# The keys' reciprocal norms written straight into their tile, and GpSimd's powers priced higher in a build-time order

## The chip, the cores and the metric

One NeuronCore of a Trainium2 chip runs the whole program. It has five engines that run side by side, each through its own list of instructions and strictly in order: TensorE (PE in the profile, with its weight loads as PEld), VectorE (DVE), ScalarE (ACT), GpSimd (POOL) and SyncE (SP), which here only issues transfers. An instruction that waits holds up everything behind it on its own engine. The metric is the device time of one execution in microseconds (us); lower is better.

## The reference

One block of a transformer on 1024 tokens of width 1024, all in fp32. The input is normed and projected; four heads go through a gated delta rule (a chunked linear recurrence), eight heads through a dilated sliding window attention; both are joined by an output projection, and a gated feed-forward layer of width 2816 follows. The change sits in the norms of the delta-rule heads:

```python
def l2norm(x):
    return x * lax.rsqrt(jnp.sum(x * x, axis=-1, keepdims=True) + 1e-6)

q = l2norm(heads(q)) * GDN_HEAD_DIM ** -0.5
k = l2norm(heads(k))
...
o = chunk_gated_delta_rule(q, k, v, g, beta)
o = o * lax.rsqrt(jnp.mean(o * o, axis=-1, keepdims=True) + RMS_EPS) * onorm_g.astype(f32)
```

## The kernel before, in words

**Who sets the order.** The kernel is written as generators ("strands"), each of which yields one instruction after the other. At build time a class named Weaver picks, step by step, the strand whose next instruction can start earliest by its own running clocks, and writes that instruction into its engine's list. The clocks advance by a cost that class Op gives to each instruction (from line 184 on), plus fixed lags between engines. Nothing of this runs on the chip: only the lists remain. So a cost that is altered alters no instruction by itself, but it alters which one is written next, and from there on every later choice can differ. Some operations are also given to one of two engines by the same clocks (Either: a cast on ACT or DVE, a sum on DVE or GpSimd).

**The stages, in order of time.** (1) The projections: each 128-column block of w_in is split into a high and a low fp32r part, and PE does three matmuls 128x512 for each of eight blocks of the depth (tiles pj). They run through the first 487 us and serve as the filler of all other work on PE in that time. (2) Beside them, for each delta-rule head: a causal convolution on DVE (tile yc, four instructions on 128x1024), the norms of queries and keys (post_q, post_k), and the chunk matrices (intra; tiles rhd, am, attnT on DVE, pm on PE). (3) When all four heads are done, inverse solves 31 triangular steps on DVE (tiles tm and X), then solve finishes on PE. (4) chain, the recurrence over 16 half-tiles: matmuls p1, p2, p3 (p in the profile), DVE tiles R, o and state in between, and for each token tile chain_out, which norms the result (tile on_r). (5) The window attention runs beside the chain, unit by unit: scores on PE (pS), bias and row minimum on DVE (Sr, mx), the exponential on ACT, four transposes on PE (tp<-ident,Sr), their split into high and low parts on ACT and DVE (ptn, pto, ptf), the product with the values on PE (pV), and two sums on DVE (plow, ptmp). (6) The output projection (pw), then the feed-forward layer (bank), which fills the second half of the time.

**The norms.** rstd_from takes sums of squares, scales them on DVE (tile ..._m) and raises them to the power -0.5 on GpSimd (tile ..._r). It is called with the tags rk (keys, 128x4, twice a head), rq (queries, 128x8, once a head), on (the chain's result, 128x4, eight times), and n3 and n4 (norms around the output projection, 128x1, sixteen times). Op prices a power at 295 + 165 n ns for n elements in a row. In post_k the result of rk is first copied on DVE into the tile rk, which holds the norms of all heads, then multiplied in place by a decay (edec), and that product scales the keys (kn).

Of the kernel before, what the change touches and what calls it, by code (L numbers as in the profile page):

```python
# [11 lines left out]
F32 = mybir.dt.float32  # L12
# [3 lines left out]
ALU = mybir.AluOpType  # L16
# [5 lines left out]
P = 128  # L22
# [8 lines left out]
EPS = 1e-6  # L31
# [508 lines left out]
def block_kernel(ctx: ExitStack, tc: tile.TileContext, a, out):  # L540
    nc = tc.nc
    w = Weaver(nc)
    T, V, A, G, SY = (Engine(w, e, k) for e, k in (
        (nc.tensor, "PE"), (nc.vector, "V"), (nc.scalar, "A"), (nc.gpsimd, "G"), (nc.sync, "S")))
# [5 lines left out]
    def tr(out, in_):  # L550
        return T.transpose(out, in_, ident[:])
# [16 lines left out]
    def pool(stack, name, bufs, space=None, side=None):  # L568
        return Pool(w, stack, tc, name, bufs, space, side)
# [11 lines left out]
    mhalf = pc.tile([P, 32], F32, name="mhalf")  # L581

    psums = pc.tile([P, NT, AH], F32, name="psums")

    def rstd_from(pool, ss, scale, eps, tag, bufs=4):
        n = ss.shape[-1]
        m = pool.tile([P, n], F32, name=tag + "_m", bufs=bufs)
        yield V.tensor_scalar(m[:], ss, scale, eps, ALU.mult, ALU.add)
        r = pool.tile([P, n], F32, name=tag + "_r", bufs=bufs)
        yield G.tensor_tensor(r[:], m[:], mhalf[:, :n], ALU.pow)  # L590
        return r

    d_kq = dr.tile([NT, P, GH, 4, 64], F32, name="d_kq")
# [23 lines left out]
    rq = pgv.tile([P, GH, NT], F32, name="rq")  # L617
# [245 lines left out]
    pk = pool(s1, "pk", 2)  # L863
# [30 lines left out]
    rk = pl.tile([P, GH, NT], F32, name="rk")  # L894
    edec = pl.tile([P, 32], F32, name="edec")
# [83 lines left out]
    def conv(raw, wi):  # L979
        raw, used = raw  # L980
        yc = yield pk.get([P, S], F32, name="yc", bufs=1)
        yield V.tensor_scalar(yc[:], raw[:, 0:S], convw[:, wi, 0:1], None, ALU.mult)
        for j in range(1, 4):
            yield V.scalar_tensor_tensor(yc[:], raw[:, j:j + S], convw[:, wi, j:j + 1], yc[:], ALU.mult, ALU.add)
        used.fire()
        return yc

    def tok_major(src, b, after):
        yield After(after)
        tp = yield pt.get([P, 4, P], F32, name="tp")  # L990
        yield [tr(tp[:, k, :], src(4 * b + k)) for k in range(4)]
        return tp

    def sumsq(tp, ss):
        sq = yield pk.get([P, 4, P], F32, name="sq4", bufs=1)
        yield A.activation(sq[:], tp[:], AF.Square)
        yield V.tensor_reduce(ss, sq[:], AX.X, ALU.add)
        pk.put(sq)
# [4 lines left out]
    def post_k(h, raw, evs):  # L1003

        for e in evs:
            yield e
        yc = yield from conv(raw, 4 + h)
        ys = yield pk.get([P, S], F32, name="ys")
        yield A.activation(ys[:], yc[:], AF.Silu)
        pk.put(yc)  # L1010
        kq = kqs[h] = yield pk.get([P, NT, 4, 64], F32, name="kq")
        y4 = ys[:].rearrange("p (t c j) -> p t c j", t=NT, c=2)
        yield Either(A.copy(kq[:, :, 0::3, :], y4), V.tensor_copy(kq[:, :, 0::3, :], y4))
        yield ev_dec
        kn = yield pk.get([P, NT, P], F32, name="kn")
        for b in range(2):
            sl = slice(4 * b, 4 * b + 4)
            tp = yield from tok_major(lambda k: ys[:, k * P:(k + 1) * P], b, ys[:])
            ss = pk.tile([P, 4], F32, name="ssk")
            yield from sumsq(tp, ss[:])  # L1020
            r = yield from rstd_from(pk, ss[:], 1.0, 1e-6, "rk")
            yield V.tensor_copy(rk[:, h, sl], r[:])
            yield V.tensor_tensor(r[:], r[:], edec[:, h * 8 + 4 * b:h * 8 + 4 * b + 4], ALU.mult)
            yield V.tensor_tensor(kn[:, sl, :], tp[:], r[:].unsqueeze(2).broadcast_to([P, 4, P]), ALU.mult)
            pt.put(tp)
        pk.put(ys)
        yield V.tensor_tensor(nbeta[:, h, :], nbeta[:, h, :], rk[:, h, :], ALU.mult)
        yield V.tensor_tensor(nbeg[:, h * 8:h * 8 + 8], nbeg[:, h * 8:h * 8 + 8], rk[:, h, :], ALU.mult)
        ev_k[h].fire()
        yield SY.dma_start(d_kd[:, :, h, :].rearrange("t p d -> p t d"), kn[:])  # L1030
        pk.put(kn)

    def post_q(h, raw, evs):
        for e in evs:
            yield e
        yc = yield from conv(raw, h)
        while h not in kqs:
            yield ev_k[h]
        kq = kqs[h]
        yield A.activation(kq[:, :, 1:3, :], yc[:].rearrange("p (t c j) -> p t c j", t=NT, c=2), AF.Silu)  # L1040
        pk.put(yc)
        ev_q[h].fire()
        ssq = pk.tile([P, 8], F32, name="ssq")
        for b in range(2):
            tp = yield from tok_major(lambda k: kq[:, k, 1:3, :], b, kq[:])
            yield from sumsq(tp, ssq[:, 4 * b:4 * b + 4])
            pt.put(tp)
        rr = yield from rstd_from(pk, ssq[:], 1.0, 1e-6, "rq")
        yield V.tensor_scalar(rq[:, h, :], rr[:], P ** -0.5, None, ALU.mult)
        yield ev_k[h]  # L1050
        yield SY.dma_start(d_kq[:, :, h, :, :].rearrange("t p c j -> p t (c j)"),
                           kq[:].rearrange("p t c j -> p t (c j)"))
        ev_kq[h].fire()
# [202 lines left out]
    def main():  # L1256
# [11 lines left out]
        for n, (kind, i) in enumerate(order):  # L1268
            if kind in ("k", "q", "v"):
                if n < 2:  # L1270
                    raw, ev = pair[n]
                else:
                    raw, ev = (yield from new_raw()), []
                    for hf in range(2):
                        e = yield from proj_half(base[kind] + i, hf, raw_sink(raw))
                        ev.append(e)
                if kind == "k":
                    ev_post.append(w.spawn(post_k(i, raw, ev), 3))
                elif kind == "q":
                    fin += [w.spawn(post_q(i, raw, ev), 3), w.spawn(intra(i), 3)]  # L1280
                    if i == GH - 1:
                        w.spawn(inverse(fin), 2)
                else:
                    ev_post.append(w.spawn(post_v(i, raw, ev), 4))
                    if i == GH - 1:
                        ev_main_v.fire()
            elif n == 2:
                continue
            elif kind == "bv":
                yield from proj_v(i)  # L1290
            elif kind == "gate":
                if i < 2:
                    yield from gate(i)
                elif i == 2:
                    yield from gate(2, 3)
            else:
                yield from proj_qk(base[kind], i, (ev_q2 if kind == "bq" else ev_k2)[i])
# [63 lines left out]
    ch = pool(sc, "ch", 2)  # L1361
# [28 lines left out]
    def chain():  # L1390
        for t in range(NT):
# [4 lines left out]
            for c in range(2):  # L1396
# [30 lines left out]
                cp.put(p2)  # L1427
            ch.put(kq, gg, kd, bv)
            w.spawn(chain_out(o, t), 3)

    def chain_o1(o, p1, sw, us):
# [4 lines left out]
    def chain_out(o, t):  # L1436
        sq = yield ch.get([P, GH, P], F32, name="osq", tag="ot", bufs=1)
        yield A.activation(sq[:], o[:], AF.Square)
        ss = ch.tile([P, GH], F32, name="oss")
        yield V.tensor_reduce(ss[:], sq[:], AX.X, ALU.add)  # L1440
        ch.put(sq)
        yield V.tensor_tensor(ss[:], ss[:], rqs2[:, t::8], ALU.mult)
        r = yield from rstd_from(ch, ss[:], 1.0, EPS, "on", 2)
        yield V.tensor_tensor(r[:], r[:], rqsw[:, t::8], ALU.mult)
        yield V.tensor_tensor(o[:], o[:], r[:].unsqueeze(2).broadcast_to([P, GH, P]), ALU.mult)
        yield After(o[:])
        tp = yield banks.get([P, GH, 2, 64], F32, name="otp")
        yield [tr(tp[:, h, :, :], o[:, h, :]) for h in range(GH)]
        ch.put(o)
        ot = yield ch.get([P, GH, 2, 64], F32, name="ot", bufs=1)  # L1450
        for c in range(2):
            yield A.activation(ot[:, :, c, :], tp[:, :, 1 - c, :], AF.Copy, scale=onorm[:])
        banks.put(tp)
        yield A.dma_start(d_mix[0:4, :, t * P:(t + 1) * P].rearrange("h p j -> p h j"),
                           ot[:].rearrange("p h c j -> p h (c j)"))
        ch.put(ot)
        ev_o[t].fire()
# [1018 lines left out]
```

## Time and the profile before

| | us |
|---|---|
| median of 3 runs (1234.30 to 1237.12) | 1235.44 |
| the profiled execution | 1238.43 |
| its span, first to last instruction | 1236.6 |
| around the span (1238.43 - 1236.6) | 1.8 |
| PE busy | 1212.7 (98%) |
| DVE busy | 967.0 (78%) |
| ACT busy | 573.4 (46%) |
| GpSimd busy | 179.8 (15%) |

The span is what the profile's views cover; the profiled execution lies 3.0 us above the median of the runs. In the views, "x18" counts instructions, the mean duration of one is in ns, and what follows "<-" is what ended an idle time.

### The profile page before, as it was taken

To read this page: it belongs to the slowest core of one execution; us is meant where nothing else is said; L and a number is where in the kernel's file an instruction comes from. 1 tells how busy PE (TensorE), PEld (TensorE's weight loads), DVE (VectorE), ACT (ScalarE), POOL (GpSimd) and SP (SyncE) were. 2 spreads that over 40 slices of the span, in tenths; PEclk is the share of its full clock that TensorE was granted. 3 is DMA by queue.
4 is the path that set the end of the run, shared out by engine and by line. 5 is a ranking of instruction groups with operands and counts; after the bars stand their busy time and mean duration, and the time that the engine had idled before them with its cause. 6 is when DMAs were issued, how large, how long until landed. Compare 5 with 4: busy or idle time off the path is not lost.

```text
span 1236.6 us, 19600 instructions
## 1 busy us (share of the span) xinstructions
PE 1212.7 (98%) x6783; PEld 1013.4 (82%) x6783; DVE 967.0 (78%) x1875; ACT 573.4 (46%) x1162; POOL 179.8 (15%) x153
## 2 busy tenths in 40 slices
PE   8999999999999999999999999999999999999997
PEld 7887798888888877887778888888888888888886
DVE  5689969736998988766898867876678767876886
ACT  6535432236676658555553333333333344544541
POOL 0134321011122111110110010111001100000111
PEclk9999999999999999999999999999999999999999
DMA  8754372778878568785544433322333039645335
GB/s 273 228 158 154 111 227 81 171 228 264 268 224 255 175 185 273 243 275 174 188 134 154 139 128 128 103 65 98 120 128 119 35 120 322 239 131 158 101 121 205
DMA packets 169979, 213.43 MB, mean 173 GB/s; under 512 B 32232, under 2 KB 87016, under 8 KB 169880
## 3 DMA queue, kind: packets, MB, share of 16 engines
q1 hardware_dynamic: 165656, 210.08, 54.0%
q10 hardware_dynamic: 4224, 2.10, 0.6%
q8 instruction: 54, 0.88, 0.3%
q14 instruction: 45, 0.37, 0.1%
HBM read 149.97 MB, written 65.95 MB: 175 GB/s over the span
## 4 chain that ended last, share of the span: by engine, by line
PE 80%; DMA 7%; DVE 6%; ACT 2%; SPq 2%; issue 1%; POOL 1%; DVEq 0%; POOLq 0%; ACTq 0%
PE bank L284 49%; PE pj L284 16%; PE pw L284 5%; PE tp L284 3%; PE p L284 3%; SPq L284 2%; PE pS L284 2%; PE pm L284 2%; PE pV L284 1%; DMA d_bias<-d_rev 1%; DMA xn<-in_x 1%; DMA y<-in_w_out 1%; DMA gt<-d_gt 0%; DVE yc L284 0%; DMA xT<-in_x_t 0%
## 5 line engine op out<-in xcount | busy, mean ns | idle before, releaser
L284 PE MATMUL pj<-hTh,w 128*128 128x512 f32 x768 | 263.9, 402 | 5.7 <-ACT hTh L284 5.7
L284 PEld LDWEIGHTS pj<-hTh,w 128*128 128x128 f32 x768 | 145.3, 189 | 37.1 <-ACT hTh L284 6.1
L284 ACT CAST wbh<-wraw 128x512 fp32r<-128x512 f32 x130 | 80.5, 622 | 198.4 <-PE bank L284 127.4
L284 PE MATMUL pj<-hTl,w 128*128 128x512 f32 x384 | 151.2, 394 | 0.0
L284 DVE TENSOR_TENSOR wbl<-wraw,wbh 128x512 fp32r<-128x512 f32 x129 | 91.9, 715 | 31.8 <-ACT wbh L284 31.7
L284 PE MATMUL bank<-views 128*128 128x512 f32 (+1 forms) x307 | 84.8, 384 | 0.0
L284 PEld LDWEIGHTS pj<-hTl,w 128*128 128x128 f32 x384 | 72.8, 190 | 12.3 <-DVE hTl L284 1.0
L284 PE MATMUL bank<-views,dah 128*128 128x512 f32 (+1 forms) x214 | 73.5, 379 | 0.0
L284 PE MATMUL bank<-dbh,views 128*128 128x512 f32 (+1 forms) x201 | 70.3, 380 | 0.0
L284 PEld LDWEIGHTS bank<-views 128*128 128x128 f32 x307 | 57.4, 188 | 11.5
L284 POOL TENSOR_TENSOR m<-m,m 128x512 f32<-128x512 f32 x18 | 28.3, 1572 | 252.0 <-DVE r L284 142.0
L284 PE MATMUL pw<-woh,mh 128*128 128x512 f32 x128 | 51.9, 405 | 0.4 <-ACT woh L284 0.4
L284 PE MATMUL pw<-wol,mh 128*128 128x512 f32 x128 | 50.1, 392 | 0.5 <-DVE wol L284 0.5
L284 PE MATMUL pw<-woh,ml 128*128 128x512 f32 x128 | 50.1, 391 | 0.0
L284 PE MATMUL bank<-dbh,dah 128*128 128x512 f32 (+1 forms) x129 | 49.1, 381 | 0.0
L284 DVE SCALAR_TENSOR_TENSOR yc<-raw,convw,yc 128x1024 f32<-128x1024 f32 x36 | 47.3, 1313 | 0.4
L284 ACT CAST w<-wr 128x512 fp32r<-128x512 f32 x53 | 32.5, 619 | 31.9 <-PE pj L284 25.0
L284 PEld LDWEIGHTS bank<-views,dah 128*128 128x128 f32 x214 | 40.0, 188 | 7.7
L284 ACT ACTIVATE Sr<-Sr,mx 128x384 f32<-128x384 f32 (+2 forms) x64 | 38.3, 599 | 15.2 <-DVE mx L284 14.1
L284 DVE TENSOR_TENSOR m<-bank,m 128x512 f32<-128x512 f32 x44 | 30.1, 685 | 18.2 <-PE bank L284 18.2
L284 PEld LDWEIGHTS bank<-dbh,views 128*128 128x128 f32 x201 | 37.6, 188 | 7.1
L284 DVE TENSOR_TENSOR w<-wr,w 128x512 fp32r<-128x512 f32 x39 | 27.1, 702 | 20.1 <-ACT w L284 20.0
(399 smaller groups left out, 3267.8 us busy)
## 6 DMA issues: line engine op xcount, KB each, us to landing
wr<-in_w_in SPq DMA_DIRECT2D x56, 256.0 KB
wraw<-in_w_gate SPq DMA_DIRECT2D x52, 256.0 KB
wraw<-in_w_up SPq DMA_DIRECT2D x52, 256.0 KB
views<-d_hid SPq DMA_DIRECT2D x47, 256.0 KB
db<-in_w_down SPq DMA_DIRECT2D x40, 256.0 KB
qs<-d_q SPq DMA_DIRECT2D x64, 128.0 KB
da<-d_hid SPq DMA_DIRECT2D x30, 256.0 KB
d_hid<-x SPq DMA_DIRECT2D x22, 256.0 KB
```

The lines of the kernel that those rows point to most:

```text
L284: op.fn(*op.args, **op.kw)
```

## The change

Three things are done. The power of rk writes straight into its place in the tile rk, so the copy on DVE (eight in all) is gone, and the product with the decay goes to a tile of its own, rk_f. rstd_from adds a fixed amount, held, to the planner's cost of the power: 760 ns for rk, 930 for rq, 50 for on, 200 for n3 and n4. And since these costs steer the Weaver, the lists of all engines are written anew from the first affected choice on.

```diff
-    def rstd_from(pool, ss, scale, eps, tag, bufs=4):
+    def rstd_from(pool, ss, scale, eps, tag, bufs=4, held=200.0, out=None):
         n = ss.shape[-1]
         m = pool.tile([P, n], F32, name=tag + "_m", bufs=bufs)
         yield V.tensor_scalar(m[:], ss, scale, eps, ALU.mult, ALU.add)
-        r = pool.tile([P, n], F32, name=tag + "_r", bufs=bufs)
-        yield G.tensor_tensor(r[:], m[:], mhalf[:, :n], ALU.pow)
+        r = pool.tile([P, n], F32, name=tag + "_r", bufs=bufs)[:] if out is None else out
+        op = G.tensor_tensor(r, m[:], mhalf[:, :n], ALU.pow)
+        op.cost += held
+        yield op
         return r
...
-            r = yield from rstd_from(pk, ss[:], 1.0, 1e-6, "rk")
-            yield V.tensor_copy(rk[:, h, sl], r[:])
-            yield V.tensor_tensor(r[:], r[:], edec[:, h * 8 + 4 * b:h * 8 + 4 * b + 4], ALU.mult)
-            yield V.tensor_tensor(kn[:, sl, :], tp[:], r[:].unsqueeze(2).broadcast_to([P, 4, P]), ALU.mult)
+            r = rk[:, h, sl]
+            yield from rstd_from(pk, ss[:], 1.0, 1e-6, "rk", out=r, held=760.0)
+            f = pk.tile([P, 4], F32, name="rk_f", bufs=4)
+            yield V.tensor_tensor(f[:], r, edec[:, h * 8 + 4 * b:h * 8 + 4 * b + 4], ALU.mult)
+            yield V.tensor_tensor(kn[:, sl, :], tp[:], f[:].unsqueeze(2).broadcast_to([P, 4, P]), ALU.mult)
...
-        rr = yield from rstd_from(pk, ssq[:], 1.0, 1e-6, "rq")
+        rr = yield from rstd_from(pk, ssq[:], 1.0, 1e-6, "rq", held=930.0)
...
-        r = yield from rstd_from(ch, ss[:], 1.0, EPS, "on", 2)
+        r = yield from rstd_from(ch, ss[:], 1.0, EPS, "on", 2, held=50.0)
```

In the built programs the lists are the same up to 78 us of the profile before, and again from about its 605 us on. PE is given the same 6139 matmuls in both (the profile counts some of them twice). DVE has 1852 instructions in place of 1877 (the eight copies are gone, and some casts went to ACT), ACT has 16 table loads in place of 20. Three places show the moves.

The first is on DVE, at the keys of the third head. Before, the product with the decay and the tile rhd, for which PE waits, stand behind the copy that waits for the power:

```order
L284 TENSOR_SCALAR rk_m<-ssk 128x4
L284 TENSOR_TENSOR am<-am,mD 128x512
L284 TENSOR_TENSOR w<-wr,w 128x512
L284 COPY rk<-rk_r 128x4
L284 TENSOR_TENSOR raw<-pj,rb 128x512
L284 TENSOR_TENSOR rk_r<-rk_r,edec 128x4
L284 TENSOR_TENSOR rhd<-g_145,mDT 128x1024
L284 TENSOR_TENSOR kn<-tp,rk_r 128x512
```

Now the same rhd (of the third head, with the mask mDT) follows the second rk_m directly, and the instruction that waits for the second power (rk_f) stands behind it:

```order
L284 TENSOR_TENSOR rk_f<-rk,edec 128x4
L284 TENSOR_TENSOR am<-am,mD 128x512
L284 TENSOR_TENSOR kn<-tp,rk_f 128x512
L284 TENSOR_REDUCE ssk<-sq_1426 128x4
L284 SCALAR_TENSOR_TENSOR yc<-raw,convw,yc 128x1024
L284 TENSOR_TENSOR raw<-pj,rb 128x512
L284 TENSOR_SCALAR rk_m<-ssk 128x4
L284 TENSOR_TENSOR rhd<-g_145,mDT 128x1024
L284 TENSOR_SCALAR yc<-raw,convw 128x1024
L284 TENSOR_TENSOR rk_f<-rk,edec 128x4
```

What moved: rhd no longer stands behind a wait for GpSimd.

The second is on DVE in the last third of the triangular steps of inverse. Before, the steps follow each other nearly undisturbed:

```order
L284 TENSOR_TENSOR X<-X,tm 128x7x25
L284 SCALAR_TENSOR_TENSOR yc<-raw,convw,yc 128x1024
L284 TENSOR_TENSOR tm<-la,X 128x156
L284 TENSOR_TENSOR X<-X,tm 128x6x26
L284 TENSOR_TENSOR tm<-la,X 128x135
L284 TENSOR_TENSOR X<-X,tm 128x5x27
L284 TENSOR_TENSOR tm<-la,X 128x112
L284 TENSOR_TENSOR X<-X,tm 128x4x28
```

Now the convolution of another value head and the scaling of its tiles stand between the same steps:

```order
L284 TENSOR_TENSOR tm<-la,X 128x135
L284 TENSOR_TENSOR raw<-pj,rb 128x512
L284 TENSOR_TENSOR kn<-tp,beta 128x512
L284 TENSOR_TENSOR X<-X,tm 128x5x27
L284 TENSOR_TENSOR kn<-tp,beta 128x512
L284 TENSOR_TENSOR tm<-la,X 128x112
L284 TENSOR_SCALAR yc<-raw,convw 128x1024
L284 TENSOR_TENSOR X<-X,tm 128x4x28
L284 SCALAR_TENSOR_TENSOR yc<-raw,convw,yc 128x1024
```

What moved: among the 31 steps stand nine of the long convolution instructions in place of three, so the solve and the chain behind it come later against the projections. Counted on PE, 777 projection matmuls 128x512 stand ahead of the chain's first matmul before, and 867 now; 117 stand behind its last one before, and 30 now.

The third is on PE, in the last part of the window attention. Before, projection matmuls (pj) stand between its pieces up to the first matmul of the output projection:

```order
L284 MATMUL pj<-hTl,w 128x512
L284 MATMUL pj<-hTh,w 128x512
L284 MATMUL tp<-ident,Sr 128x128 x11
L284 MATMUL pj<-hTh,w 128x512
L284 MATMUL pj<-hTl,w 128x512
L284 MATMUL pj<-hTh,w 128x512 x2
L284 MATMUL pj<-hTl,w 128x512
L284 MATMUL pj<-hTh,w 128x512
L284 MATMUL pV<-ptn,vn 128x2x128 x3
```

Now the projections have run out there, and from the last of them to the first pw there are 149 attention matmuls (29 tp, 74 pS, 46 pV) and four transposes of the chain, one behind the other:

```order
L284 MATMUL tp<-ident,Sr 128x128 x9
L284 MATMUL pS<-ks,qs_5302 128x256
L284 MATMUL pS<-ks,qs_5333 128x256
L284 MATMUL pS<-ks,qs_5302 128x256
L284 MATMUL pS<-ks,qs_5333 128x256
L284 MATMUL pS<-kf,qf 32x128 x8
L284 MATMUL pV<-ptn,vn 128x2x128 x3
L284 MATMUL pV<-ptn,vn 128x2x64
L284 MATMUL pV<-pto,vo 128x2x128
L284 MATMUL pS<-ks,qs_5523 128x256
```

What moved: the filler of this stretch now stands ahead of the chain.

## The prediction

> **What bounds the kernel now.** I read the page first, then who PE waits for, then the stretches in which it waits.
>
> ```profile
> PE 1212.7 (98%) x6783; PEld 1013.4 (82%) x6783; DVE 967.0 (78%) x1875; ACT 573.4 (46%) x1162; POOL 179.8 (15%) x153
> ```
>
> PE is busy for 1212.7 us of a span of 1236.6, so all that any order can win back is the 23.9 us in which it is not, and its matmuls are the same before and after. The view of PE's waits says where part of these 23.9 us lie:
>
> ```profile
> PE pj L284 <- ACT hTh L284: 5.7, 1, 5.7
> PE pm L284 <- DVE rhd L284: 2.2, 2, 1.7
> PE tp L284 <- DVE y L284: 2.1, 2, 1.3
> PE pS L284 <- DVE ptn L284: 1.6, 1, 1.6
> PE bank L284 <- DVE wbl L284: 1.5, 1, 1.5
> ```
>
> Total us, how often, the longest. The 5.7 us are the start of the program and stay. The others wait for DVE: it is the second bound, and it decides where PE stands still. The windows (length, then busy time of PE, PEld, DVE, ACT, GpSimd, and so on) show where:
>
> ```profile
> 300.00:320.00 20.00, 18.91 (x149) 16.15 (x148) 17.75 (x53) 12.62 (x33) 2.79 (x3) 1.00 0.81 262
> 320.00:340.00 20.00, 19.80 (x170) 16.68 (x170) 18.90 (x61) 13.31 (x39) 3.70 (x4) 1.00 0.84 252
> 440.00:460.00 20.00, 18.39 (x140) 15.54 (x139) 17.19 (x59) 12.66 (x39) 2.77 (x3) 1.00 0.70 210
> 460.00:480.00 20.00, 19.69 (x158) 15.35 (x157) 16.69 (x57) 13.96 (x29) 1.40 (x4) 1.00 0.96 276
> 480.00:500.00 20.00, 19.55 (x133) 15.91 (x132) 18.62 (x51) 15.93 (x41) 4.24 (x3) 1.00 0.83 250
> 600.00:620.00 20.00, 19.17 (x89) 15.62 (x89) 19.86 (x34) 13.89 (x28) 3.53 (x3) 1.00 0.45 147
> ```
>
> While chain and attention run, DVE is busy 17 to 19 of every 20 us, and yet PE loses little, because projection matmuls fill its list between the pieces that wait for DVE.
>
> **The change, part by part.** *The powers.* The copy behind them first (smallest, median and largest duration in ns):
>
> ```profile
> L284 DVE COPY rk<-rk_r x8: 151/160/1239, 97.0 to 158.0; 128x4 f32<-128x4 f32 x8
> ```
>
> It takes 0.16 us as a rule and 1.24 once. The timeline shows that once, the place where the powers reach PE (start and length in us, and in brackets the idle time ahead):
>
> ```profile
> 124.70 1.98 POOL L284 TENSOR_TENSOR rk_r<-rk_m,mhalf 128x4 f32<-128x4 f32 x1 [9.27 <-DVE rk_m L284]
> 126.65 1.28 POOL L284 TENSOR_TENSOR w<-wr,w 128x512 fp32r<-128x512 f32 x1
> 126.71 1.24 DVE L284 COPY rk<-rk_r 128x4 f32<-128x4 f32 x1 [0.90 <-POOL rk_r L284]
> 128.53 1.21 DVE L284 TENSOR_TENSOR rhd<-g,mDT 128x1024 fp32r<-128x1024 f32 x1
> 129.89 0.70 PE L284 MATMUL pm<-rhd,tgtr 128*128 128x512 f32 x2 [1.66 <-DVE rhd L284]
> ```
>
> DVE idles 0.90 us for the power; then the copy takes 1.24 us in place of its median 0.16, and ends at 127.95, when GpSimd's sum on w ends (126.65 + 1.28 = 127.93). These 0.90 + 1.08 = 1.98 us push rhd, and PE waits 1.66 us for it. In the new list rhd stands ahead of the instruction that waits for the power, so I take **-1.7 us**. Bounds: 0, if another wait takes its place, and -2.2, both waits for rhd.
>
> A rule is weighed here. The Trainium skill (SBUF — State Buffer, section "Who interferes with whom") says that VectorE and GpSimd share a pair of ports by an exclusive lock, taken by copies, and that VectorE instructions with two SBUF inputs contend with GpSimd instructions that read SBUF. The stretched copy above agrees. By it the product rk_f, which has two such inputs and takes the copy's place behind the power, can be held up in the same way, and this term would be 0 in place of -1.7.
>
> Beside the waits, eight copies (1.3 us of DVE at the median 0.16) and four table loads of ACT go. ACT is busy 46% and DVE had other work to reach: I cost both at nothing.
>
> *The chain moves against the filler.* 90 more projection matmuls stand ahead of the chain (867 against 777). One takes 0.229 us on PE, from this row of the chain that ended last:
>
> ```profile
> 133.08 5.49 PE pj L284 x24
> ```
>
> (5.49 / 24), so chain and attention begin some 20.6 us later. That alone costs nothing, since PE does the same work in another order. In the chain the filler stays (255 against 258), so I take 0; bounds -1.3 (the 1.09 + 0.20 us that PE lost from 300 to 340, all gone) and +1.3 (as much again).
>
> *The stretch without filler* is the main term. From the last projection matmul to the first pw, PE has attention alone. I take the part from the end of its first ten pV to its last sixteen pV, which wait for the split parts pto. DVE has 50 instructions in it, all of which lie behind a plow that waits for those ten pV. Their mean durations (third number, ns), for 290 to 520 us:
>
> ```profile
> L284 DVE TENSOR_TENSOR ptn<-tp,ptn 128x256 fp32r<-128x256 f32 x56 | 22.3, 416 | 1.7 <-ACT ptn L284 1.1
> L284 DVE TENSOR_TENSOR ptmp<-pV,plow 64x256 f32<-64x256 f32 x31 | 19.7, 636 | 1.0
> L284 DVE CUSTOM_DVE_ANT_0 Sr<-pS,strip 128x256 f32<-128x256 f32 x40 | 15.7, 416 | 1.5 <-PE pS L284 1.3
> L284 DVE TENSOR_TENSOR plow<-pV,plow 64x256 f32<-64x256 f32 x31 | 12.7, 409 | 2.3 <-ACT plow L284 2.2
> L284 DVE CUSTOM_DVE_ANT_0 Sr<-pS,strip,mx 128x128 f32<-128x128 f32 x32 | 10.5, 343 | 0.1
> L284 DVE TENSOR_TENSOR pto<-tp,pto 128x128 fp32r<-128x128 f32 x32 | 8.7, 282 | 0.4
> L284 DVE TENSOR_TENSOR qf<-qs,qs 128x512 f32<-128x512 f32 x12 | 8.4, 702 | 3.5 <-DMA qs<-d_q 3.5
> L284 DVE CUSTOM_DVE_ANT_0 Sr<-pS,strip 128x512 f32<-128x512 f32 x8 | 5.5, 687 | 1.6 <-PE pS L284 1.5
> ```
>
> The list has 10 splits ptn (4.2 us), 6 ptmp (3.8), 4 Sr of 256 (1.7), 6 plow (2.5), 4 Sr,mx (1.4), 11 splits of 128 columns (3.1), 2 qf (1.4), 2 Sr of 512 (1.4) and 5 small ones, at some 0.34 each an estimate from the 282 and 416 rows (1.7): 21.2 us. One begins about 0.07 us before the one ahead ends (453.21 + 0.41 against 453.55), except behind the six plow, so 44 x 0.07 = 3.1 us come off: **18 us**. DVE's timeline has that, and two rows for later:
>
> ```profile
> 446.94 0.41 DVE L284 TENSOR_TENSOR plow<-pV,plow 64x256 f32<-64x256 f32 x1
> 450.23 0.43 DVE L284 CAST spread<-wor 128x512 fp32r<-128x512 f32 x1 [2.20 <-DMA wor<-in_c_spread]
> 453.21 0.41 DVE L284 TENSOR_TENSOR ptn<-tp,ptn 128x256 fp32r<-128x256 f32 x1
> 453.55 0.41 DVE L284 CUSTOM_DVE_ANT_0 Sr<-pS,strip 128x256 f32<-128x256 f32 x1
> ```
>
> PE's own work there follows from the starts in its timeline:
>
> ```profile
> 444.05 0.63 PE L284 MATMUL pS<-ks,qs 128*128 128x256 f32 x4
> 444.62 0.65 PE L284 MATMUL pS<-kf,qf 128*32 128x128 f32 x16
> 445.27 0.66 PE L284 MATMUL pV<-ptn,vn 128*128 128x256 f32 x4
> 445.77 0.34 PE L284 MATMUL pV<-pto,vo 128*128 128x256 f32 x1
> 445.95 0.39 PE L284 MATMUL pj<-hTh,w 128*128 128x512 f32 x1
> 462.60 1.07 PE L284 MATMUL pS<-kf,qf 128*32 128x256 f32 x16
> 463.60 0.68 PE L284 MATMUL pV<-ptn,vn 128*128 128x256 f32 x4
> 466.02 1.36 PE L284 MATMUL tp<-ident,Sr 128*128 128x128 f32 x11
> 467.13 0.48 PE L284 MATMUL pj<-hTh,w 128*128 128x512 f32 x1
> ```
>
> A transpose costs (467.13 - 466.02) / 11 = 0.10, so 29 cost 2.9. A group of five pV costs 445.95 - 445.27 = 0.68, so four cost 2.7. Of the scores, four near ones cost 0.57, eight far ones (x16 in the rows, which hold two records of each) 0.57 at 128 columns or 1.0 at 256: with 20 near, 24 and 16 of these, 2.9 + 1.7 + 2.0 = 6.6. In all 12.2 us against DVE's 18, and before DVE can begin, the first plow passes ACT: 446.94 - (445.77 + 0.34) = 0.8 us behind its pV. PE therefore stands still for about 18 + 0.8 - 12.2 = 6.6 us. Its losses in the same part before were 1.61 + 0.31 + 0.45 = 2.4 us in the three windows from 440 to 500; the 1.6 of them that waited for ptn came behind the late transfer of spread (DVE idle 2.20 us at 450.23), which stays, so 0.8 go. Net 6.6 - 0.8 = **+5.8 us**. Bounds: +2.2, if DVE gets through in a fifth less than its means say (14.4 for 18), and +7.8, if the splits wol of the first pw, which DVE now reaches only behind that stretch, cost another 2 us.
>
> **The sum** is -1.7 + 0 + 5.8 = +4.1 us: a span of 1240.7 in place of 1236.6, a profiled execution of 1242.5 in place of 1238.43. The runs lie 3.0 lower (median 1235.44), which gives **1239.5 us**.
>
> **The rivals.** (A) *The delay is absorbed later.* Behind 600 us both lists are the same, and PE waits there for DVE (19.86 of 20 us busy): 2.1 for y and 1.5 for wbl. If PE comes later while DVE does not, these 3.6 us shrink: 4.1 - 3.6 = +0.5, so 1235.9. Against it: DVE is what makes PE late, and comes late itself. (B) *Faster.* The filler that now stands ahead of the chain lets DVE run ahead, so the stretch loses no more than the 2.4 us of before; with both rhd waits (-2.2) and the losses of 300 to 340 us (-1.3) gone, -3.5, so 1231.9. It decides when PE idles less than 2.4 us between the last pj and the first pw. For it: DVE has 25 instructions fewer. (C) *The powers keep their wait* because rk_f stands where the copy stood: the term -1.7 falls away, +5.8, so 1241.2. The rule on the ports above would do just this.
>
> **How the numbers follow.** Within 0.2% (2.5 us, about what a measurement of this kernel can tell from no change) is 1232.9 to 1237.9. I give my forecast 0.42, (C) 0.12, (A) 0.28, (B) 0.18. Forecast and (C) are slower, 0.54, but the forecast lies only 1.6 us beyond the limit, so 0.05 of it count as the same: faster 0.18, same 0.33, slower 0.49. The bounds of the terms add up to -2.2 - 1.3 + 2.2 = -1.3 and 0 + 1.3 + 7.8 = +9.1, that is 1234.1 to 1244.5; I draw the lower end to 1232.9, where faster begins, so that little more than (B) is left out. Forecast and (C) alone span 1237 to 1244.5.
>
> **What would show it.** In the profile after: no wait of pm for rhd behind rk (if it is there, the first step is wrong); PE waits of several us in all for DVE (Sr, ptn, pto, ptf or wol) between the last pj and the first pw, where PE's window falls to about 15 of 20 us; DVE near 19 of 20 there. If PE's idle there is small, the main term is wrong; if it is as said and the time still equals that of before, (A) is right.

## The result, and the profile after

The changed kernel takes 1251.99 us (median of 5 runs, 1247.98 to 1253.66) and the kernel before, on the same chip, 1237.12 (5 runs, 1234.3 to 1239.42): the ratio is 1.0117, with a 95% interval of 1.0103 to 1.013. That is 14.9 us more, slower as forecast, but 12.5 us over the predicted time and past the upper end of the range. The profiled execution took 1253.66 us with a span of 1251.9, against 1238.43 and 1236.6.

Whom PE waits for, in the changed kernel, behind the 5.6 us at its start (total us, how often, the longest; ... marks a line left out):

```profile
PE tp L284 <- ACT Sr L284: 5.0, 3, 3.8
PE tp L284 <- DVE y L284: 3.0, 3, 1.7
PE pV L284 <- DMA vo<-d_v: 2.5, 1, 2.5
PE tp L284 <- ACT ys L284: 1.6, 2, 1.0
PE bank L284 <- DVE wbl L284: 1.5, 1, 1.5
PE pS L284 <- DMA ks<-d_k: 0.8, 1, 0.8
PE pS L284 <- ACT kf L284: 0.8, 1, 0.8
PE pw L284 <- DVE wol L284: 0.7, 1, 0.7
...
PE pm L284 <- DVE rhd L284: 0.6, 1, 0.6
```

New are the waits for vo, ys, ks and kf, and the one for Sr has grown from 0.2 us. The wait of 1.7 us for rhd is gone; one of 0.6 us lies at 106.8 us, at the keys of another head. Where time is lost, the windows of the changed kernel show (length, then busy time of PE, PEld, DVE, ACT, GpSimd; then granted clock of PE, DMA share, GB/s):

```profile
260.00:380.00 120.00, 119.97 (x981) 102.32 (x975) 80.66 (x224) 68.28 (x175) 24.40 (x24) 1.00 0.77 239
380.00:460.00 80.00, 79.80 (x640) 69.65 (x639) 72.86 (x230) 58.80 (x163) 13.28 (x13) 1.00 0.66 202
460.00:480.00 20.00, 14.82 (x126) 10.98 (x124) 11.97 (x44) 12.21 (x31) 0.77 (x2) 0.83 0.70 210
480.00:500.00 20.00, 14.14 (x89) 9.99 (x89) 15.27 (x53) 16.00 (x43) 3.84 (x3) 0.80 0.90 246
460.00:520.00 60.00, 48.22 (x335) 36.09 (x334) 45.17 (x139) 43.05 (x110) 10.32 (x9) 0.86 0.81 240
```

and in the kernel before:

```profile
260.00:380.00 120.00, 118.36 (x883) 101.17 (x882) 94.67 (x274) 73.52 (x192) 25.09 (x25) 1.00 0.82 252
380.00:460.00 80.00, 78.39 (x613) 68.03 (x612) 72.60 (x232) 53.02 (x155) 13.09 (x13) 1.00 0.67 196
460.00:520.00 60.00, 58.39 (x392) 47.03 (x391) 50.74 (x141) 41.52 (x97) 8.74 (x9) 1.00 0.84 257
```

Up to 460 us the changed kernel is ahead. From 460 to 520 PE is busy 48.22 us at a clock of 0.86, some 41.5 us of work at full clock, against 58.4 before: by that estimate 17 us lost in one place. DVE is not near its limit there, busy 11.97 and 15.27 of 20 us. One row more stands out, in the window from 260 to 380: PE has more to do (119.97 against 118.36 us) while DVE does 14 us less (80.66 against 94.67). Some 7 of these 14 us DVE never does in this kernel: its busy time in all is 959.8 us, 967.0 before. The other half it still has to do at 460. The timeline says why it is late. In the kernel before, the first and last instruction of the inverse's 31 steps on DVE, the first matmul of solve and the first of the chain stand at (start, length in us):

```profile
178.99 0.20 DVE L284 TENSOR_TENSOR tm<-la,X 128x31 f32<-128x31 f32 x1
215.84 0.18 DVE L284 TENSOR_TENSOR X<-X,tm 128x31 f32<-128x31 f32 x1
234.85 1.20 PE L284 MATMUL pm<-uz,a 32*32 32x32 f32 x64
276.80 1.13 PE L284 MATMUL p<-R,cg 128*128 128x128 f32 x8 [0.17 <-issue]
```

and in the changed kernel at:

```profile
187.17 0.20 DVE L284 TENSOR_TENSOR tm<-la,X 128x31 f32<-128x31 f32 x1
234.19 0.19 DVE L284 TENSOR_TENSOR X<-X,tm 128x31 f32<-128x31 f32 x1
253.87 1.20 PE L284 MATMUL pm<-uz,a 32*32 32x32 f32 x64
296.29 1.05 PE L284 MATMUL p<-R,cg 128*128 128x128 f32 x8
```

The run of the inverse begins 8.2 us later and takes 47.2 us in place of 37.0, since 30 other instructions of DVE (26.0 us) stand in it where 20 (15.3 us) did. Solve starts 19.0 us later, the chain 19.5. PE, with projections to do all the while, shows next to no gap until they are used up: the two waits for ys, at 223 and 234 us, are 1.6 of the 1.9 us that it loses between 180 and 460.

### The profile page after: what moved, and what is told of

Its sections match the earlier page's. It is cut to its first block, busy times and chain, and to the rows that moved or that the text cites. A ratio compares the mean times of both kernels' runs of the same rounds, so it can differ in the third digit from the quotient of the medians.

```text
span 1251.9 us, 19594 instructions
## 1 busy us (share of the span) xinstructions
PE 1220.1 (97%) x6783; PEld 1018.9 (81%) x6783; DVE 959.8 (77%) x1850; ACT 573.8 (46%) x1177; POOL 178.8 (14%) x151
## 4 chain that ended last, share of the span: by engine, by line
PE 84%; DVE 7%; DMA 5%; issue 1%; ACT 1%; SPq 0%; POOL 0%; DVEq 0%; POOLq 0%; ACTq 0%
PE bank L284 48%; PE pj L284 22%; PE tp L284 4%; PE p L284 3%; PE pw L284 3%; PE pm L284 2%; PE pS L284 2%; PE pV L284 1%; DVE x L284 1%; DMA mx<-d_mix 1%; DMA gpost<-in_w_out 1%; DMA y<-in_w_out 1%; DMA x<-in_x 1%; DMA d_x<-x 0%; DMA gt<-d_gt 0%
## 5 line engine op out<-in xcount | busy, mean ns | idle before, releaser
L284 PEld LDWEIGHTS pj<-hTl,w 128*128 128x128 f32 x384 | 72.8, 190 | 12.5 <-DVE hTl L284 0.8
L284 POOL TENSOR_TENSOR w<-wr,w 128x512 fp32r<-128x512 f32 x17 | 23.0, 1351 | 164.0 <-ACT w L284 162.0
L284 ACT ACTIVATE Sr<-Sr,mx 128x384 f32<-128x384 f32 (+2 forms) x64 | 38.2, 597 | 12.5 <-DVE mx L284 12.1
```

The costliest lines, as they stand in the source:

```text
L284: op.fn(*op.args, **op.kw)
```

## The experiments

Each run is compared with the kernel before on its own chip. Differences below are median minus median; "alone" counts the attention matmuls between the last pj and the first pw in the program's order, solve is the start of its first matmul, and "chain ends" is the start of the chain's last matmuls, both in us from the start of the profiled span.

| run | us | ratio to before, 95% | difference | alone | solve | chain ends |
|---|---|---|---|---|---|---|
| before | | | 0 | 0 | 234.8 | 431.7 |
| changed kernel | 1251.99 | 1.0103 to 1.013 | +14.9 | 149 | 253.9 | 451.1 |
| e1_code_only | 1235.71 | 0.9966 to 0.9988 | -2.7 | 0 | 237.4 | 430.6 |
| e2_prices_only | 1257.13 | 1.013 to 1.0179 | +18.8 | 176 | 260.6 | 458.9 |
| e3_rk_unpriced | 1246.49 | 1.004 to 1.0081 | +8.1 | 37 | 245.2 | 443.5 |
| e4_rq_unpriced | 1247.25 | 1.0053 to 1.0118 | +8.9 | 37 | 243.8 | 443.3 |
| e8_filler_kept | 1248.04 | 1.0075 to 1.0119 | +11.7 | 0 | 252.9 | 439.7 |
| e14_before_inverse_late | 1257.48 | 1.0121 to 1.0167 | +19.6 | 176 | 260.0 | 460.1 |
| e15_after_pairs | 1247.79 | 1.0066 to 1.012 | +10.5 | 37 | 245.9 | 445.1 |
| e16_after_twos | 1239.83 | 1.0007 to 1.0034 | +2.5 | 0 | 246.0 | 438.7 |

### The change taken apart

The direct write without prices, the prices without the direct write, and the changed kernel with one price back:

```diff
# e1: held=0.0 everywhere, out=rk[:, h, sl] stays
# e2: the copy stays
-            yield from rstd_from(pk, ss[:], 1.0, 1e-6, "rk", out=r, held=760.0)
+            r = yield from rstd_from(pk, ss[:], 1.0, 1e-6, "rk", held=760.0)
+            yield V.tensor_copy(rk[:, h, sl], r[:])
...
# e3: held=760.0 -> 0.0        e4: held=930.0 -> 0.0
```

> The direct write of the norms alone, every price as before. In its order 78 projection matmuls stand behind the chain's last transposes (96 before, none in the changed kernel) and no attention matmul stands between the last projection matmul and the first of the output projection (149 in the changed kernel). Theory F (the stretch without filler makes the loss): the copy's 1.2 us and the wait of pm for rhd behind it go, nothing is lost later: 1233 to 1237 us, same or a little faster than before. Rival W (the direct write itself costs, by GpSimd writing the kept tile or the later readers): most of the 14.9 us is here, 1245 to 1252.

> The four prices alone, the copy kept. The order has 176 attention matmuls between the last projection matmul and the first of the output projection. Theory F: the loss goes by the length of that stretch: 14.9 us lost and about 2.4 won by the powers over 149 matmuls is some 17 us, times 176 / 149 is 20, less what the prices alone win near the powers (0 to 1): 1254 to 1260 us. Rival W: without the direct write the time is that of before, 1235 to 1240.

> The changed kernel with the price of the keys' power as before; queries 930 and the norms 200 and 50 stay. 37 attention matmuls stand between the last projection matmul and the first of the output projection, 54 projection matmuls behind the chain. Theory F, if the loss is in proportion: 17 x 37 / 149 is 4 us, less about 2 won: 1237 to 1241 us. If the loss begins only past what PE's queue of finished scores can bridge: 1234 to 1237. Rival P (the keys' price in itself puts the powers wrong): 1235, and the run with the queries' price taken out 1250.

> The changed kernel with the price of the queries' power as before; keys 760 and the norms stay. Again 37 attention matmuls without filler. Theory F: the same as the run with the keys unpriced within 2 us, 1234 to 1241. Rival P: about 1250, since the keys' price stays.

The direct write alone is faster than before (-2.7 us, and its interval leaves 1 out), so rival W falls; it is also the fastest kernel of the study. All of the loss comes with the prices. With either of the two large ones taken out 8 to 9 us are still lost, so P falls too. The small prices, 50 and 200, stood in both runs and were not tried alone. But 37 matmuls alone cost far more than in proportion: theory F had 1241 at most.

### Inside the stretch without filler

The longest wait, on ScalarE's timeline of the changed kernel:

```profile
463.02 1.28 ACT L284 ACT_TABLE_LOAD   x1
464.32 1.15 ACT L284 ACTIVATE gst<-gst 128x512 f32<-128x512 f32 x2
...
467.66 1.28 ACT L284 ACT_TABLE_LOAD   x1
468.96 0.61 ACT L284 ACTIVATE Sr<-Sr,mx 128x384 f32<-128x384 f32 x1
```

The silu of the last gate, with a table load on either side, stands between scores that DVE had finished and their exponential; in the part left out ACT also idles 1.19 us for DVE. PE's transposes wait 3.78 us. Then the clock falls: in the changed kernel's windows of 5 us

```profile
465.00:470.00 5.00, 1.22 (x10) 1.02 (x10) 2.83 (x7) 3.78 (x8) 0.21 (x1) 0.80 0.61 190
470.00:475.00 5.00, 4.97 (x34) 3.93 (x33) 2.98 (x10) 2.58 (x11) 0.00 (x0) 0.52 0.77 180
```

PE is busy 4.97 us behind the wait, at half clock. And loads come late: SP's queue waited for loads of the output weights (y and gpost) to land, 2.1 us of it ahead of vo (from the view of SP's waits, 460 to 500 us):

```profile
SPq L284 <- DMA y<-in_w_out: 3.0, 2, 1.7
SPq L284 <- PE pS L284: 2.9, 1, 2.9
SPq L284 <- DMA d_mix<-ptmp: 2.9, 1, 2.9
SPq L284 <- DMA gpost<-in_w_out: 2.1, 1, 2.1
```

Three runs take one of these away each, the fourth all three:

```diff
# e5: ahead of the transposes that wait for Sr (30), and of the values that wait for vo (20)
+                nc.tensor.transpose(dst, ident[:], ident[:])
# e6: the last two gate tiles are copied, and their silu is left out
-        yield [A.activation(z[:], z[:], AF.Silu) for z, _ in part]
...
+                op.fn = lambda o, i, f: nc.scalar.activation(o, i, AF.Copy)
# e7: half of the load, the left half used for both
-            yield SY.dma_start(wr[:], a["w_out"][k])
+            op.fn = lambda o, i: nc.sync.dma_start(o[:, 0:512], i[:, 0:512])
# e10: e5 (10 and 8), e6 and e7 together
```

> The changed kernel with 50 transposes of the identity that nothing reads: 30 ahead of PE's transposes of Sr that waited 3.8 us, 20 ahead of the products of the values that waited 2.5 us for vo, each some 0.12 us, so PE works through most of the two waits. Theory G (the granted clock, which fell to about 0.52 behind each of these waits, makes a large part of the loss): the 5 us behind the first wait and the 6 us behind the second run at full clock, some 2.5 and 2.5 us shorter: 1246 to 1249 us. Theory L (the stretch goes by the latencies of the other engines and of the loads, and a slow PE only fills what would be idle): 1251 to 1254 us, the clock near 1 all the same.

> The changed kernel with the last two gate tiles left as they are (a copy in place of their silu), so ScalarE loads no table between the scores' exponentials at 463 and 468 us (two loads of 1.28 us). Theory S (the silu of the last gate stands between finished scores and their exponential once no filler covers it): PE's wait of 3.8 us falls to 1.0 to 1.6, and with it the fall of the clock behind it is smaller: 1246 to 1250 us. If the loss is elsewhere: 1251 to 1253.

> The changed kernel with the first four blocks of the output projection's weights loaded by half (256 KB in place of 512 each) and the left half used for both. Theory D (the loads of the attention stand behind these in SP's queue, which waited 5.1 us for y and gpost to land between 470 and 491 us): the waits of SP halve, vo comes earlier and PE's wait of 2.5 us for it shrinks below 1: 1247 to 1250 us. If the loads do not set the end: 1251 to 1253.

> The changed kernel with three cuts at once in the stretch without filler: no silu on the last two gate tiles, the first four blocks of the output weights loaded by half and the left half used twice, and 18 transposes of the identity (10 and 8) ahead of the two long waits. If the gains of the single runs (1.4 and 1.9, and 0 by the transposes) add up: 1248 to 1249.5 us. If the waits stand in for one another, so that only all of them together shorten the stretch: 1242 to 1247.

Measured: e5 1252.34 us (ratio 1.01 to 1.0139), e6 1250.61 (1.0092 to 1.013), e7 1250.13 (1.0085 to 1.0122), e10 1250.48 (1.0091 to 1.0131): +14.5, +12.7, +12.2 and +14.2. In e5 the same two windows are

```profile
465.00:470.00 5.00, 4.55 (x41) 4.58 (x42) 3.39 (x15) 3.77 (x7) 0.00 (x0) 1.00 0.72 230
470.00:475.00 5.00, 3.62 (x35) 2.36 (x34) 2.54 (x8) 3.56 (x14) 0.21 (x1) 1.00 0.71 166
```

The clock stays at 1.00, PE idles instead (3.62 of 5 us busy), and the time is the same. So theory G falls for the first of its two waits: the slow clock there only fills what would be idle. Behind the second wait the clock fell in e5 too, to 0.52 from 500 to 505 us, so that part of G was not tested. In e6 the waits for Sr fall from 5.0 to 2.4 us and one of 1.6 us for ptn is new; in e7 the wait for vo grew, from 2.5 to 3.0 us. The intervals of all four overlap that of the changed kernel, and the three cuts do not add up: e10 is slower than either range it was given. No single wait of those that were cut makes the loss. The stretch is where the loss shows.

### Filler put back

The changed kernel, with the last gate halves held back by hand (e9 releases them earlier):

```diff
+                if (h, hf) in held_back:
+                    yield held_back[h, hf]
                 yield from proj_half(12 + h, hf, lambda hf, ps, h=h: sink(h, hf, ps))
...
+    held_back = {(2, 0): ev_out[6], (3, 0): ev_out[7], (2, 1): ev_att[6][0], (3, 1): ev_att[7][0]}
```

> The changed kernel, all its prices and the direct write, with four halves of the last two gates' projections (96 matmuls) held back by hand until the chain's outputs 6 and 7 and the attention of heads 6 and 7 have been issued. The order is that of the changed kernel up to there; behind the chain's last transposes stand 87 projection matmuls (0 in the changed kernel), and no attention matmul stands between the last of them and the first of the output projection. Theory F: the loss of the stretch goes, what the powers won stays: 1233 to 1239 us. Rival E (the loss comes from the earlier part, where the prices moved the powers and the inverse): 1248 to 1253.

> The same with the halves released earlier: 63 projection matmuls behind the chain's last transposes, 24 attention matmuls without filler. Theory F: between the run with 87 and the two runs with 37 (1246.5 and 1247.3): 1236 to 1246 us. Rival E: 1248 to 1253.

Both miss theory F, and both lie where rival E has them: +11.7 and +15.0 us (e9: 1251.3 us, ratio 1.0101 to 1.0141). No attention matmul stands alone in e8, and still only 3 us of 14.9 come back. Its windows:

```profile
380.00:460.00 80.00, 73.13 (x607) 61.82 (x606) 72.76 (x237) 53.89 (x158) 15.73 (x16) 1.00 0.64 190
460.00:520.00 60.00, 56.31 (x387) 44.16 (x388) 53.37 (x148) 45.20 (x109) 7.99 (x7) 1.00 0.86 269
```

The stretch is healed (56.31 of 60 busy, clock 1.00), and PE idles from 380 to 460 instead, 6.9 of 80 us where it was 0.2. There the filler that was held back is missing: among others PE waits 3.4 us for the chain itself (vn, R and state). Theory F in its simple form falls: the hole moves with the filler. What stays in e8 is the delay of what the filler has to cover (solve at 252.9). That this delay makes the size of the hole is not shown by e8, since the hold itself alters where PE stands still; the next runs test it.

### The delay of the inverse

Theory C: the loss is the delay of the serial run inverse, solve, chain, attention. e14 makes that delay alone, in the kernel before; e11, e15 and e16 shorten the run in the changed kernel by issuing its steps in groups (of 4, 1 and 2), e12 and e17 with the direct write alone (4 and 1), e13 in the kernel before (4).

```diff
# e14: in inverse(), and in main() where the projection bk0 is reached
+        yield ev_held
+            if n == 11:
+                ev_held.fire()
# e16 (two steps at a time)
...
+            ops += [V.tensor_tensor(tv, ...), V.tensor_tensor(X[:, k + 1:, 0:m], ...)]
+            if k % 2 == 1 or k == 30:
+                yield ops
+                ops = []
```

> The kernel before, its powers, prices and copy as they were, with the inverse alone held back until the projection bv1 has been issued, so that 117 more projection matmuls stand ahead of the chain, as with the prices alone (e2). Theory C: the loss of the change without any of its parts, about that of e2: 1250 to 1260 us. If the powers' prices lose by anything but the delay of the inverse: 1235 to 1240.

> The changed kernel, with the 31 steps of the inverse issued on VectorE in groups of four, so that other instructions of VectorE come only between groups. Theory C (the loss is the delay of the serial run inverse, solve, chain, attention): the steps themselves take 21 us of the 47.0, the rest is 30 other instructions between them; with some 8 of them left the run takes 28 to 32 us, solve starts 15 to 19 us earlier than at 253.9, and 0.8 of that comes off the time: 1234 to 1240 us. Rival Q (VectorE held for 2.7 us at a time leaves PE without free pj banks, or solve isn't what is waited for): 1246 to 1255.

> The direct write alone with the inverse in the same groups of four. Theory C: solve starts some 8 us earlier than at 237.4: 1228 to 1234 us. Rival Q: 1236 or more.

> The kernel before with the inverse in the same groups of four and nothing else. Theory C: its run takes 29 us where it took 36.3, solve starts 7 us earlier than at 234.8: 1230 to 1235 us. Rival Q: 1237 or more.

> The changed kernel with the two instructions of each step of the inverse issued as a pair, so that others come only between steps: 20 others in the run where 30 were. Theory C: the run takes 38 to 40 us in place of 47.0, solve starts 8 us earlier than at 253.9, and no waits of PE for pj are added: 1243 to 1248 us. If the delay of solve does not matter: 1251 to 1253.

> The changed kernel with the inverse in groups of two steps: 15 other instructions in the run. Theory C: the run takes some 34 us, solve starts at about 241, 13 us earlier, with 0 to 3 us of waits for pj: 1240 to 1246 us. If the stalls of the groups cost as much as the earlier solve gains: 1248 to 1252.

> The direct write alone with the inverse's steps in pairs: 12 others in the run where 21 were, so some 31 us where it took 39.0. Theory C, if solve alone sets the chain's start: 8 us earlier, 1229 to 1233 us. If the values' part, which is pushed behind the inverse, sets the chain's start as in the run with groups of four (281.0): 1234 to 1240.

e14 has the powers, prices and copy of before, and loses 19.6 us, as much as the prices alone (18.8). The delay brings 176 matmuls without filler with it, as there, so e14 shows what the delay costs together with what follows from it, not the one without the other. Its timeline and window:

```profile
192.54 0.20 DVE L284 TENSOR_TENSOR tm<-la,X 128x31 f32<-128x31 f32 x1
240.49 0.18 DVE L284 TENSOR_TENSOR X<-X,tm 128x31 f32<-128x31 f32 x1
259.98 1.20 PE L284 MATMUL pm<-uz,a 32*32 32x32 f32 x64
```

```profile
460.00:520.00 60.00, 44.99 (x327) 33.63 (x326) 47.40 (x150) 40.46 (x107) 6.22 (x6) 0.83 0.81 246
```

A start 13.6 us later became 25.1 at solve, because the run fell among the convolutions of the value heads, and the hole opened at 460 us, some 270 us behind its cause. In the other direction, e16 in the changed kernel:

```profile
224.74 0.19 DVE L284 TENSOR_TENSOR X<-X,tm 128x31 f32<-128x31 f32 x1
...
245.95 1.20 PE L284 MATMUL pm<-uz,a 32*32 32x32 f32 x64
```

```profile
180.00:260.00 80.00, 73.63 (x579) 59.08 (x580) 65.22 (x115) 15.18 (x21) 7.81 (x6) 0.98 0.48 121
460.00:520.00 60.00, 56.29 (x388) 43.38 (x388) 53.78 (x147) 45.42 (x108) 8.82 (x8) 1.00 0.84 270
```

Solve is 7.9 us earlier than in the changed kernel (13 were forecast), and of the 14.9 us 2.5 are left, though the groups cost PE new waits (73.63 of 80 us busy from 180 to 260, 78.37 in the changed kernel).

Of the other groupings, e15 (+10.5) came in at the upper end of theory C's range, and the rest missed it; the three in groups of four ended where rival Q has them. e11 brought solve back to 235.2 and the stretch to 59.06 of 60 us busy, but ended at 1246.41 (ratio 1.0034 to 1.0075), as DVE, held for four steps, kept PE from free pj banks (from 180 to 260 pj waited 5.2 us for DVE, and PE was busy 74.60 of 80 us). e12 (1245.0; 1.0039 to 1.0081) and e13 (1250.87; 1.0072 to 1.0117) had solve at 225.9 and 225.4 and were slower than the kernels they came from: the chain still began at 281.0 and 286.3. e17 (1245.57; 1.0053 to 1.0098) had solve at 233.5 and the chain at 277.5, 3 us earlier than e1, and lost 11 us against it. Part of that is new waits of PE from 180 to 260 (busy 76.27 of 80, e1 79.98). Another part, some 3.8 us by an estimate from busy time and clock, lies from 460 to 520 (55.90 at 0.91, e1 54.71 at 1.00), where PE waits 2.7 us for pto; the rest we can't place. And e15 and e16 start solve at the same time, 8 us apart in the result: in e15 37 attention matmuls stand alone, in e16 none. So how much filler is left counts as well, and one number for solve doesn't give the time.

The end of the chain orders the runs better. e3, e4, e15 and e16 start solve within 2.2 us of each other, but their chains end at 443.5, 443.3, 445.1 and 438.7 us, and they lose 8.1, 8.9, 10.5 and 2.5 us. All runs of the table follow this order within 1 us, but for e8, in which filler was held by hand. Outside of it stand also e9, the groups of four, and e17, whose chain ends at 427.5 us. This is an order read from one profile of each run; no experiment moved the end of the chain by itself, and which choice of the Weaver let the convolutions into the inverse is not followed here.

## Why the prediction was wrong

- *The powers, -1.7 us.* Right in size. The wait behind the stretched copy is gone, and the windows from 0 to 100 and from 100 to 180 us have PE busy 94.36 and 79.13 us where it was 93.87 and 77.82: 1.8 us won; the direct write alone won 2.7. But the sign "no wait of pm for rhd behind rk" failed at another place. At the keys of the first head rhd stands directly behind rk_f, which took 1.25 us there (its median is 0.16), as long as GpSimd was at its sum on w:

```profile
104.19 1.29 POOL L284 TENSOR_TENSOR w<-wr,w 128x512 fp32r<-128x512 f32 x1 [1.60 <-ACT w L284]
104.25 1.25 DVE L284 TENSOR_TENSOR rk_f<-rk,edec 128x4 f32<-128x4 f32 x1
105.43 1.21 DVE L284 TENSOR_TENSOR rhd<-g,mDT 128x1024 fp32r<-128x1024 f32 x1
106.78 0.69 PE L284 MATMUL pm<-rhd,tgtr 128*128 128x512 f32 x2 [0.61 <-DVE rhd L284]
```

So what rival (C) names did happen, once in eight, and cost PE 0.6 us; its price, the whole 1.7, did not come. The prediction also took the copy to be stretched once; in the kernel before it was twice, to 1.24 and, at 100.29 us, to 0.67.
- *The chain moves against the filler, 0.* **This step failed**, in the sentence "That alone costs nothing, since PE does the same work in another order." The delay itself was foreseen (20.6 us, measured 19.5 at the chain's first matmul). But PE's work is not all that must be done: the inverse, solve, the chain and the attention follow one another, and when they start later, less filler is left to cover them; by 380 us DVE, too, stood some 7 us of work behind. A kernel with a delay of this kind and none of the change's parts (e14) lost 19.6 us, and with the run of the inverse shortened in the changed kernel (e16) 2.5 of the 14.9 us were left.
- *The stretch without filler, +5.8 us.* Right place and sign, mis-sized: PE did some 17 us less work there than before, and its windows fell to 14.82 and 14.14 us where about 15 of 20 was forecast. I took the stretch to go at the pace of DVE (18 us of its instructions), and it went by a chain of short waits for ACT, DVE and loads, with DVE busy 12 to 15 of 20 us. The sign "DVE near 19 of 20" failed. But a better price for this stretch would have missed the cause too: with the filler back in it (e8), 11.7 us were still lost.
- *(A), absorbed later,* did not happen: PE's waits for y and wbl, 2.1 and 1.5 us before, are 3.0 and 1.5 after. (Of the 2.1 us, 1.3 stood at 569 us, not behind 600, so (A) had less to win than it says.) *(B), faster,* needed an idle PE below 2.4 us between the last pj and the first pw; from 460 to 520 PE idles 11.8 us.
- The sum by these steps: +1.8 from the powers, -16.9 from 460 to 520, +1.6 and +1.4 won by filler from 260 to 380 and 380 to 460, and -1.6 lost from 180 to 260 (78.37 busy, 80.00 before) make 13.7 of the 15.3 us between the two spans.

## What to carry to other kernels

In this kernel an engine that is always busy hid a delay of the serial run behind it, until its filler was gone. So look not only at its gaps but at when each long dependent run starts, and price a start that moves as a loss unless something absorbs it. When a hole appears, ask what ran late long ahead of it (here some 270 us); filling the hole by hand only moved it. Prices that are nearer to the profile can make a greedy order worse: here the direct write alone was faster than before, and rating the powers nearer to what they take cost 17.6 us on top (14.9 + 2.7).

## What was unexpected of the hardware

The granted clock fell during the wait of PE of 3.78 us (465.9 to 469.7) and was 0.52 in the 5 us from 470, and 1.00 again in the 5 us behind those. The Trainium skill (TensorE: Matmul & The Clock Gate, section "Part 1: The HAM clock gate") states two rates, half and full, decided over windows of some 3.4 us of idle or busy PE; the trace agrees on the two rates: windows of 1 us read 1.00 or 0.50, but for those in which the clock changes. An idle window of that length was not needed here:

```profile
467.00:468.00 1.00, 0.00 (x0) 0.00 (x0) 0.51 (x2) 0.70 (x2) 0.00 (x0) 1.00 1.03 359
468.00:469.00 1.00, 0.00 (x0) 0.00 (x0) 0.97 (x3) 0.99 (x2) 0.00 (x0) 0.51 0.61 198
489.00:490.00 1.00, 0.81 (x4) 0.84 (x4) 0.93 (x5) 0.45 (x4) 0.00 (x0) 0.50 0.98 209
```

At 468 us PE had been idle for 2.1 us. Ahead of the fall at 489, PE was busy 2.72 of the 5 us from 483 to 488, at a clock of 1.00, and waited for 0.84 us at the longest. The first fall cost nothing: e5 kept the clock at 1.00 behind that wait by transposes that nobody reads, and the time stayed.

A transfer's issue on SP can wait for a transfer issued eight places ahead: ahead of vo, the queue waited 2.1 us for gpost, and gpost, four qs, two ks and one strip stand before vo in its list. Whether the queue itself or the program's semaphores ask for that, no run shows.
